# A conformer/SSD block on one core: the re-ordered hand-over with adding loads for block sums, and two token tiles transposed with the identity

## The chip, the core and the metric

The kernel runs on one core of a Trainium2 chip. The core has a matrix engine (TensorE, "PE" in the profile, with its weight loads "PEld"), and three engines for element-wise work: VectorE (DVE), ScalarE (ACT) and GpSimd (POOL). SyncE (SP), ScalarE and GpSimd also issue transfers (DMAs), each in its own queue. Each engine takes its instructions in a fixed order, and an instruction waits for semaphores that others raise. The metric is the device time of one execution in microseconds (us).

## The reference, cut to what matters

The block normalises x, mixes it in two branches (a convolution and a state-space scan), projects the mix with `w_out`, adds it to x, and then runs the feed-forward part. All data are float32: 512 tokens, width 1024, hidden width 2816. Only the seam between the projection and the feed-forward part is touched:

```python
mixed = (g_conv * conv_out + g_ssm * ssm_out) @ w_out[i]
x = x + rms_norm(mixed, mix_post_g[i])
h = rms_norm(x, ffn_pre_g[i])
gt, up = jnp.split(h @ w_gate_up[i], 2, axis=-1)
f = (jax.nn.silu(gt) * up) @ w_down[i]
x = x + rms_norm(f, ffn_post_g[i])
```

## The kernel before

**Precision.** Every large product is made of three matmuls on split numbers: each operand is a "hi" half (a cast to fp32r, ScalarE) and a "lo" half (the rest, a subtraction on VectorE). `mm3` (line 184) issues hi x hi, hi x lo and lo x hi. A lo half can be made another way: ScalarE writes the negated hi half, and GpSimd issues a transfer that adds the weight from memory to it (`halve`, line 927, for the blocks named in `ADD_LO`, line 78; the profile shows it as `wlo_g<-in_w` on POOL).

**Weights.** `w_raw` (line 142) loads pieces of 128 x 1024 (512 KB) in the order of `ORDER` through SP, into a ring of five tiles (`raw`) and later two more (`raw2`). A piece is loaded when a tile of the ring is free.

**The output projection.** `tm_wo` sums 512 tokens in four token tiles t = 0 to 3 of 128, each in two PSUM banks; the operand lies in the tiles m0h, m0l (tokens of t = 0, 1) and m1h, m1l (t = 2, 3) of the pool `mp`. The loop over `steps` (line 1080) runs t = 0 and 1 first, then 2, then 3. After the last step of a tile comes `residual(t)` (line 991): the mean of squares (ScalarE, `mean_sq`, tiles jk), the product with the gain (VectorE, `mg`), the factor (`factor`, line 869: a sum `pm` on VectorE, then a power -1/2 on GpSimd, `rs_a`), the new x (`xr`, VectorE), its mean of squares, the second factor (`rs_b`), and a diagonal matrix `dg` = identity x factor (VectorE). `xr` is loaded and then stored for the end (`x2d`) by ScalarE's queue.

**The hand-over.** `transposed(t)` (line 1014) multiplies the eight 128 x 128 pieces of xr with dg, which scales and transposes in one go (`ptr`, line 1023). The first four results go to VectorE (`xg`), the other four to ScalarE, both times with the gain of the norm. The feed-forward product uses a Strassen-Winograd scheme on 2 x 2 blocks, so hi and lo halves (`halved`, line 1037) are made of b11, b21 (from t = 0 and 2), b22 and t1 to t4 (sums, from t = 1 and 3). In the loop, `transposed(0)` stands after step (2, 1), `transposed(1)` after (2, 5) and `transposed(2)` after (3, 5).

**The block sums.** The 22 column blocks u of `w_gate_up` (gate and up in turn) come as two pieces, 2u with the upper blocks a11 | a12 and 2u + 1 with the lower ones a21 | a22. `prep_a(u)` makes hi and lo of a11, a12. `prep_s(u)` (line 949) makes four sums on VectorE, s1 = a21 + a22, s3 = a11 + a21, s2 = s1 + a11, s4 = s2 + a12, s1 in a tile of its own and the others in place of the raw pieces, and then their halves.

**The products.** `first(u)` (line 1124) starts with b11, b21 and the upper blocks. For u = 0, 1, 2 it runs before `transposed(3)`, for 3 behind it. Then per u come v1 (s1 x t1), x2 (s2 x t2), v2 (s4 x b22, into the bank of v1), x3 (s3 x t3) and x4 (a22 x t4). Between two products into one bank the bank is copied out to `D_[u]`: that is `sg` for the gates and the tile `f32[:, 2f + i]` for the up half:

```python
product(V[u], u, "s1", "t1", True)
act.copy((D_[u][1] if u in D_ else begin(u)[1])[:, c2], V[u])
```

The order for the first blocks is written out: "v0 x0 v1 w0 y0", "x1 w1 z0 y1" and so on, with v = v1, x = x2, w = v2, y = x3, z = x4. The pool `fp` of f32 is opened after `mix.close()`, so its memory lies where the pool `mp` was.

**What sets the order.** A scheduler orders each engine's instructions; `not_before` adds an order without a wait, `hold` keeps the halves behind the residual's work, `tc.issue_after` sets a place behind an instruction.

## Time and profile before

| | us |
|---|---|
| median of 3 runs (1030.25 to 1030.38) | 1030.28 |
| profiled execution, its time | 1036.17 |
| profiled execution, its span | 1034.4 |
| PE busy | 1024.2 |
| VectorE busy | 814.3 |
| ScalarE busy | 609.0 |
| GpSimd busy | 96.4 |

The profiled execution is a run of its own, some 6 us longer than the timed ones. Times in a row of the timeline count from the start of the span. The number behind the start is the duration of one instruction (of all of them, where x is above 1); matmuls overlap their predecessors, so the distance between two starts says what one costs. In the groups, the form is line, engine, operation, output <- inputs.

### The profile page before, as it was taken

The page shows a single profiled execution, that of the slowest core. Times are in us where ns is not written, and L with a number is a line of the kernel's source. Part 1 is how long each engine was busy: PE and PEld are TensorE (multiplying, and loading weights), DVE is VectorE, ACT ScalarE, POOL GpSimd, SP SyncE. Part 2 cuts the span into 40 slices and gives each one's busy share as a digit, 9 for nine tenths or more (in the row PEclk, how much of TensorE's full clock was granted, in tenths as well). Part 3 has the DMA queues.
Part 4 walks back from the last instruction along what each step waited for, and adds up shares of the span by engine and source line. Part 5 has one row for each costly group of instructions (what it writes and reads, how often), then busy time and mean ns, then how long its engine had stood idle before and what let it go on. Part 6 is the DMA issues. An engine that isn't in the chain of part 4 may idle for free.

```text
span 1034.4 us, 15686 instructions
## 1 busy us (share of the span) xinstructions
PE 1024.2 (99%) x6089; PEld 890.9 (86%) x6089; DVE 814.3 (79%) x1184; ACT 609.0 (59%) x1032; POOL 96.4 (9%) x122
## 2 busy tenths in 40 slices
PE   9999999999999999999999999999999999999997
PEld 7898889888888888888888888889999999998885
DVE  7899976959594979398976455579997788799874
ACT  7655776575748464844532673366665565568552
POOL 0101101110111011101100000010000000001000
PEclk9999999999999999999999999999999999999999
DMA  8567634655546454644452223433565345469622
GB/s 298 156 164 213 165 81 140 184 157 148 135 131 163 124 157 128 163 122 122 110 133 84 82 85 99 183 105 121 167 184 157 105 143 146 123 197 278 214 82 82
DMA packets 42458, 150.82 MB, mean 146 GB/s; under 512 B 4880, under 2 KB 5904, under 8 KB 41360
## 3 DMA queue, kind: packets, MB, share of 16 engines
q1 hardware_dynamic: 30672, 104.66, 29.9%
q0 software_dynamic: 9504, 38.80, 19.0%
q10 hardware_dynamic: 2208, 6.36, 1.8%
q8 instruction: 48, 0.79, 0.3%
q14 instruction: 26, 0.21, 0.1%
HBM read 145.54 MB, written 4.26 MB: 145 GB/s over the span
## 4 chain that ended last, share of the span: by engine, by line
PE 93%; DVE 3%; ACT 2%; issue 1%; DMA 0%; POOL 0%; SPq 0%; ACTq 0%; POOLq 0%; DVEq 0%
PE xy L187 4%; PE xy L186 4%; PE xy L188 4%; PE pz L187 3%; PE pz L188 3%; PE pz L186 3%; PE pso L186 3%; PE pso L187 3%; PE pso L188 3%; PE px L188 3%; PE px L187 3%; PE px L186 3%; PE yv L187 2%; PE yv L188 2%; PE yv L186 2%; PE yd L636 2%
## 5 line engine op out<-in xcount | busy, mean ns | idle before, releaser
L152 ACT CAST whi<-raw 128x1024 fp32r<-128x1024 f32 (+2 forms) x116 | 115.0, 1003 | 157.3 <-PE pso L187 37.5
L444 DVE SCALAR_TENSOR_TENSOR a<-v,prm_t,a 128x511 f32<-128x511 f32 (+15 forms) x240 | 179.8, 752 | 16.1 <-ACT a L441 13.8
L158 DVE TENSOR_TENSOR wlo<-raw,whi 128x1024 fp32r<-128x1024 f32 (+2 forms) x76 | 85.8, 1134 | 42.8 <-ACT whi L152 42.1
L156 POOL DMA_DIRECT2D wlo<-in_w x40 | 35.7, 893 | 353.5 <-ACT wlo L155 120.9
L188 PE MATMUL pz<-whi,hlo 128*128 128x512 f32 (+2 forms) x160 | 56.3, 352 | 0.0
L187 PE MATMUL pz<-wlo,hhi 128*128 128x512 f32 (+2 forms) x160 | 56.1, 351 | 0.0
L186 PE MATMUL pz<-whi,hhi 128*128 128x512 f32 (+2 forms) x160 | 55.4, 353 | 0.0
L186 PE MATMUL px<-hhi,whi 128*128 128x512 f32 x128 | 50.2, 392 | 0.0
L186 PE MATMUL pso<-yh,whi 128*128 128x512 f32 x128 | 50.0, 393 | 0.0
L188 PE MATMUL px<-hhi,wlo 128*128 128x512 f32 x128 | 49.8, 389 | 0.0
L187 PE MATMUL px<-hlo,whi 128*128 128x512 f32 x128 | 49.8, 389 | 0.0
L187 PE MATMUL pso<-yl,whi 128*128 128x512 f32 x128 | 49.7, 390 | 0.0
L188 PE MATMUL pso<-yh,wlo 128*128 128x512 f32 x128 | 49.7, 389 | 0.0
L930 ACT CAST whi_g<-raw 128x1024 fp32r<-128x1024 f32 x40 | 41.3, 1053 | 13.7 <-PE yv L187 8.6
L528 DVE SCALAR_TENSOR_TENSOR x<-px,prm_t,x 128x511 f32<-128x511 f32 (+2 forms) x48 | 34.7, 741 | 13.8 <-ACT x L526 13.8
L935 DVE TENSOR_TENSOR wlo_g<-raw,whi_g 128x1024 fp32r<-128x1024 f32 x34 | 41.1, 1218 | 5.1 <-ACT whi_g L930 4.7
L155 ACT ACTIVATE wlo<-whi 128x1024 fp32r<-128x1024 f32 x40 | 42.2, 1055 | 0.3
L426 ACT ACTIVATE L<-L,nacs 128x128 f32<-128x128 f32 x128 | 38.8, 389 | 0.5 <-POOL L L419 0.4
L186 PEld LDWEIGHTS pz<-whi,hhi 128*128 128x128 f32 x160 | 30.2, 189 | 3.9
L187 PEld LDWEIGHTS pz<-wlo,hhi 128*128 128x128 f32 x160 | 30.2, 188 | 3.8
L188 PEld LDWEIGHTS pz<-whi,hlo 128*128 128x128 f32 x160 | 30.1, 188 | 3.7
L930 ACT CAST chi_g<-raw 128x1024 fp32r<-128x1024 f32 x24 | 24.8, 1050 | 11.4 <-PE yv L187 5.1
(656 smaller groups left out, 3344.8 us busy)
## 6 DMA issues: line engine op xcount, KB each, us to landing
raw<-in_w SPq DMA_DIRECT2D x186, 512.0 KB, 4.5
wlo<-in_w POOLq DMA_DIRECT2D x40, 512.0 KB, 6.8
L<-scr POOLq DMA_DIRECT2D x8, 1024.0 KB, 7.1
wlo_g<-in_w POOLq DMA_DIRECT2D x11, 512.0 KB, 7.1
clo_g<-in_w POOLq DMA_DIRECT2D x7, 512.0 KB, 5.3
xr<-in_x ACTq DMA_DIRECT2D x4, 512.0 KB, 4.7
x2d<-xr ACTq DMA_DIRECT2D x4, 512.0 KB, 2.9
xres<-x2d SPq DMA_DIRECT2D x4, 512.0 KB, 3.7
```

The source lines that it names most:

```text
L152: act.copy(hi[:, c], src[:, c])
L155: act.activation(lo[:, c], hi[:, c].bitcast(F32), AF.Copy, scale=-1.0)
L156: mark["lo"] = pool.dma_start(lo[:, c], w[n][:, c].bitcast(F32R), accum_op=ALU.add)
L158: mark["wlo"] = dve.tensor_tensor(out=lo[:, c], in0=src[:, c], in1=hi[:, c].bitcast(F32), op=ALU.subtract)
L186: mark["pe"] = pe.matmul(ps, lh, rh, start=start, stop=False, skip_group_check=more)
L187: pe.matmul(ps, lh, rl, start=False, stop=False, skip_group_check=more)
L188: mark["pe3"] = pe.matmul(ps, ll, rh, start=False, stop=stop, skip_group_check=more)
L426: act.activation(L[:, h, c, :], L[:, h, c, :], AF.Exp, bias=nacs[:, c, HG * g + h : HG * g + h + 1])
L444: return dve.scalar_tensor_tensor(out=va[j][:, d:], in0=vs[j][:, : T - d], scalar=col("dw_w", j * KC + KC - 1 - d), in1=va[j][:, d:], op0= ...
L528: dve.scalar_tensor_tensor(out=a[:, d:], in0=ps[:, : T - d], scalar=col("ssm_w", i * KS + KS - 1 - d), in1=a[:, d:], op0=ALU.mult, op1=ALU ...
L930: a_ = act.copy(hi, src)
L935: d_ = dve.tensor_tensor(out=lo, in0=src, in1=hi.bitcast(F32), op=ALU.subtract)
```

## The change

- **Block sums by adding loads.** For u = 1 and 2, s1 is loaded (a21, `load_s1`, SP) and a22 is added to it by a transfer of GpSimd (`add_s1`); s3 is made by adding a11 to the raw lower piece (`add_s3`, GpSimd). VectorE keeps the sums s2 and s4. The lower pieces of u = 1 and 2 are no longer loaded into the ring: they go into a tile `b12`, in the memory of m1h, and s1 of u = 2 into that of m1l, both after the projection's last step. Block 4 joins `ADD_LO`.
- **Tiles 0 and 1** are scaled by ScalarE (two halves `xs`) and transposed with the identity (`pe.transpose`), without dg. Tiles 2 and 3 stay as they were.
- **The hand-over re-ordered.** Squares of tiles 1 to 3 stand behind earlier copies; hold marks are moved; `transposed(1)` is issued behind a matmul; `sums()` of tile 3 comes ahead of `begin(0)`; `begin(1)` is made early, into a tile `d1`. The second half of D_[1] is f32[:, 1], taken when v1(1) is reached; results of the up half go out through `f_out`.

In the built program the transposes of tile 1 stand ten matmuls later than before, those of tile 2 behind the last matmul of the projection instead of ten ahead of it.

```diff
-ADD_LO = (2, 3) + tuple(range(7, FF // P, 2))
+ADD_LO = (2, 3, 4) + tuple(range(7, FF // P, 2))
...
+    late = {}
...
-        if n < len(ORDER) and n not in raws:
-            if more_raw and n >= GU[0] and n % 7 < 2:
+        if n < len(ORDER) and n not in raws and late.get(n, True) is not None:
+            if n in late:
+                raws[n] = late[n]
+            elif more_raw and n >= GU[0] and n % 7 < 2:
...
-        pool.tensor_tensor(out=rs, in0=m, in1=neg_half[:, :1], op=ALU.pow)
+        mark["pow"] = pool.tensor_tensor(out=rs, in0=m, in1=neg_half[:, :1], op=ALU.pow)
...
+    s1s = {}
+
+    def load_s1(u):
+
+        if u == 1:
+            s1s[u] = w2.tile([P, T], F32, tag="s1", bufs=2, name=f"s1_{u}")
+        else:
+            s1s[u] = mp.tile([P, T], F32, tag="m1l", name=f"s1_{u}")
+        nc.sync.dma_start(s1s[u], w[seq["gu", 2 * u + 1]][:, :T])
+
+    def add_s1(u):
+
+        return pool.dma_start(s1s[u], w[seq["gu", 2 * u + 1]][:, T:], accum_op=ALU.add)
+
+    def add_s3(u):
+
+        return pool.dma_start(g_raw(u, 1)[:, :T], w[seq["gu", 2 * u]][:, :T], accum_op=ALU.add)
...
-        s1_ = w2.tile([P, T], F32, tag="s1", bufs=2, name=f"s1_{u}")
-        sum_ = dve.tensor_tensor(out=s1_, in0=a21, in1=a22, op=ALU.add)
+        if u in s1s:
+            s1_ = s1s[u]
+        else:
+            s1_ = w2.tile([P, T], F32, tag="s1", bufs=2, name=f"s1_{u}")
+            sum_ = dve.tensor_tensor(out=s1_, in0=a21, in1=a22, op=ALU.add)
+            if u == 3:
+                not_before(sum_, mark["t4"][1])
+            dve.tensor_tensor(out=a21, in0=a11, in1=a21, op=ALU.add)
+        sum_ = dve.tensor_tensor(out=a11, in0=s1_, in1=a11, op=ALU.add)
         if hold:
             not_before(sum_, hold[1])
-        dve.tensor_tensor(out=a21, in0=a11, in1=a21, op=ALU.add)
-        dve.tensor_tensor(out=a11, in0=s1_, in1=a11, op=ALU.add)
         dve.tensor_tensor(out=a12, in0=a11, in1=a12, op=ALU.add)
...
+            if u == 0:
+                hold[1] = mark["dg"]
             halve(("s3", "a22"), u, rb_, pair_of_tiles())
...
+    b12_raw = [seq["gu", 2 * u + 1] for u in (1, 2)]
+    late.update({n: None for n in b12_raw})
...
             ss.append(mean_sq(ps[n], pbp, f"a{t}", n))
-            m = dve.tensor_tensor(out=mg[:, c], in0=ps[n], in1=gpost0[:, c], op=ALU.mult)
-        if t == 3:
-            hold += [mark["sq"], m]
+            if t:
+                not_before(mark["sq"], mark["xg" if t > 1 else "xs"])
+            dve.tensor_tensor(out=mg[:, c], in0=ps[n], in1=gpost0[:, c], op=ALU.mult)
+        first_sq = mark["sq"]
...
+        if t == 3:
+            hold += [first_sq, m]
         rs = factor(ss, f"b{t}")
-        dg = pbp.tile([P, P], F32, tag="dg", name=f"dg{t}")
-        mark["dg"] = dve.tensor_scalar(out=dg, in0=ident, scalar1=rs, scalar2=None, op0=ALU.mult)
-        xrs[t] = xr, dg
+        if t < 2:
+            xs = [w2.tile([P, T], F32, tag=tg, bufs=2, name=f"xs{t}_{tg}") for tg in ("dhi", "dlo")]
+            for n, c in enumerate(cols2):
+                mark["xs"] = act.activation(xs[n], xr[:, c], AF.Copy, scale=rs)
+            xrs[t] = xs
+        else:
+            dg = pbp.tile([P, P], F32, tag="dg", name=f"dg{t}")
+            mark["dg"] = dve.tensor_scalar(out=dg, in0=ident, scalar1=rs, scalar2=None, op0=ALU.mult)
+            xrs[t] = [xr[:, c] for c in cols2]
+            dgs[t:] = [dg]
...
-                m = pe.matmul(pt[:, k, :], xr[:, c], dg, start=True, stop=True)
+                src = xrs[t][n][:, k * P : (k + 1) * P]
+                if t < 2:
+                    m = pe.transpose(pt[:, k, :], src, ident)
+                else:
+                    m = pe.matmul(pt[:, k, :], src, dgs[t], start=True, stop=True)
...
         if (t, k) == (2, 5):
-            sums, others = transposed(1)
+            with tc.issue_after(mark["pe"].ins):
+                sums, others = transposed(1)
             sums()
...
+        if (t, k) == (3, 2):
+            load_s1(1)
+        if (t, k) == (3, 6):
+            not_before(add_s1(1), mark["pow"])
...
-        if e == 0:
+        if u == 1:
+            d1 = h2e.tile([P, T], F32, tag="d1", bufs=1, name="d1")
+            D_[u] = [d1, None]
+        elif e == 0:
...
+    room = mp.tile([P, 2, 1024], F32, tag="m1h", name="b12")
+    for i, n in enumerate(b12_raw):
+        late[n] = room[:, i]
+        w_raw(n)
+    load_s1(2)
     halves()
-    hold[1] = mark["pm"]
     mark["chain"] = True
     for u in range(3):
         first(u)
         if u == 0:
+            hold[1] = mark["pm"]
             halves = prep_s(1)
+    for u in (1, 2):
+        not_before(add_s3(u), mark["pow"])
+    add_s1(2)
     sums, rest = transposed(3)
...
+    sums()
     begin(0)
-    sums()
     rest()
+    begin(1)
...
+    def f_out(u, i):
+        return f32[:, u - 1 + i, :] if u % 2 else D_[u][i]
...
         product(V[u], u, "s1", "t1", True)
+        if u == 1:
+            D_[u][1] = f32[:, 1, :]
         act.copy((D_[u][1] if u in D_ else begin(u)[1])[:, c2], V[u])
...
-            dve.tensor_tensor(out=d, in0=d, in1=sg[f][0], op=ALU.mult)
+            dve.tensor_tensor(out=f_out(u, 0), in0=d, in1=sg[f][0], op=ALU.mult)
```

More of the change, by code (lines that the diff above doesn't have):

```diff
@@ L1005, in residual @@
         for n, c in enumerate(cols2):
-            dve.scalar_tensor_tensor(out=xr[:, c], in0=mg[:, c], scalar=rs, in1=xr[:, c], op0=ALU.mult, op1=ALU.add)
+            m = dve.scalar_tensor_tensor(out=xr[:, c], in0=mg[:, c], scalar=rs, in1=xr[:, c], op0=ALU.mult, op1=ALU.add)
             ss.append(mean_sq(xr[:, c], pbp, f"b{t}", n))
+        if t == 3:
+            hold += [first_sq, m]
         rs = factor(ss, f"b{t}")
-        dg = pbp.tile([P, P], F32, tag="dg", name=f"dg{t}")
-        mark["dg"] = dve.tensor_scalar(out=dg, in0=ident, scalar1=rs, scalar2=None, op0=ALU.mult)
-        xrs[t] = xr, dg
+        if t < 2:
[8 more added lines that the diff above has]
+            dgs[t:] = [dg]
         nc.scalar.dma_start(x2d[t * P : (t + 1) * P, :], xr)
@@ L1016, in transposed @@
         tok = slice((t // 2) * P, (t // 2 + 1) * P)
-        xr, dg = xrs[t]
         xg = []
@@ L1021, in transposed @@
             for k in range(KB):
-                c = slice((KB * n + k) * P, (KB * n + k + 1) * P)
-                m = pe.matmul(pt[:, k, :], xr[:, c], dg, start=True, stop=True)
+                src = xrs[t][n][:, k * P : (k + 1) * P]
[3 more added lines that the diff above has]
+                    m = pe.matmul(pt[:, k, :], src, dgs[t], start=True, stop=True)
                 if t >= 2:
@@ L1034, in transposed @@
                 for k in range(KB):
-                    act.activation(xg[n][:, k], pt[:, k], AF.Copy, scale=prm_t[:, FPG + KB + k : FPG + KB + k + 1])
+                    mark["xg"] = act.activation(
+                        xg[n][:, k], pt[:, k], AF.Copy, scale=prm_t[:, FPG + KB + k : FPG + KB + k + 1]
+                    )
         def halved(name, src, sign=1.0):
@@ L1173, in x3 @@
         f, e = u // 2, u % 2
-        d = D_[u][1][:, c2]
+        d, to = D_[u][1][:, c2], f_out(u, 1)[:, c2]
         product(X[u], u, "s3", "t3", False)
@@ L1179, in x3 @@
         else:
-            gated_by(d, d, sg[f][1][:, c2])
+            gated_by(to, d, sg[f][1][:, c2])
     def v2(u):
@@ L1198, in x4 @@
         else:
-            gated_by(d, X[u], sg[f][1][:, c1])
+            gated_by(f_out(u, 1)[:, c1], X[u], sg[f][1][:, c1])
     def gated_by(out_, src, by):
```

## The prediction

> **What bounds the kernel now.** I read the page's totals first, then the busy time by stretch around the change, then the waits of TensorE (PE).
>
> ```profile
> span 1034.4 us, 15686 instructions
> PE 1024.2 (99%) x6089; PEld 890.9 (86%) x6089; DVE 814.3 (79%) x1184; ACT 609.0 (59%) x1032; POOL 96.4 (9%) x122
> ...
> 710.00:715.00 5.00, 4.58 (x40) 4.39 (x40) 4.90 (x10) 3.55 (x8) 0.00 (x0) 1.00 0.02 3
> ...
> 735.00:785.00 50.00, 50.00 (x427) 50.00 (x426) 47.20 (x72) 31.84 (x49) 1.75 (x2) 1.00 0.60 176
> ```
>
> The columns after the stretch are its length and the busy time of PE, weight load, VectorE (DVE), ScalarE (ACT), GpSimd (POOL). PE is the bound nearly everywhere: from 735 on it has no gap. Only at the hand-over from the output projection to the feed-forward part (about 697 to 729 us) does it stand, and there VectorE is the full engine (4.90 of 5.00). So a microsecond that PE loses or gains up to 729 stays to the end, and one saved on another engine counts only if PE had waited for it.
>
> ```profile
> PE xy L186 <- DVE f L1107: 0.8, 2, 0.4
> PE v L187 <- DVE t1l L1041: 0.4, 1, 0.4
> ```
>
> Those are the plain waits after 697 us. They are small, so the change has little to win and its new waits decide.
>
> **Part 1: two tiles transposed with the identity.**
>
> ```profile
> 585.96 1.13 PE L804 MATMUL pv<-ident,lxn 128*128 128x128 f32 x8
> ...
> 693.76 1.95 PE L1023 MATMUL ptr<-dg,xr 128*128 128x128 f32 x16
> 695.46 0.48 PE L188 MATMUL tm_wo<-whi,m1l 128*128 128x512 f32 x1
> ```
>
> A tile now costs 16 passes and 1.70 us of PE (693.76 to 695.46). The layer norm's transposes by the identity are the same operation on the same shape: 8 are 8 passes, 1.13 us with the tail of the last (0.28), so 0.85. Two tiles save 2 x 0.85 = 1.70 us. In return ScalarE scales two halves per tile (about 0.52 each) and VectorE drops two diagonals. The scaled halves of tile 0 fit before PE arrives, and those of tile 1 too, because their transposes stand ten matmuls later in the new order; I cost them at nothing. If the factor of tile 1 came more than about 0.7 us late, PE would wait for the excess.
>
> **Part 2: tile 2's transposes move behind the last matmul of the output projection.** Before, they stood ten matmuls ahead of it, and their copies ran under those.
>
> ```profile
> 697.60 0.39 PE L188 MATMUL tm_wo<-whi,m1l 128*128 128x512 f32 x1
> ...
> 698.18 0.39 PE L187 MATMUL xy<-b11l,a01h 128*128 128x256 f32 x1
> ...
> 699.66 0.28 PE L187 MATMUL xy<-b21l,a01h 128*128 128x256 f32 x1
> ...
> 694.85 0.69 DVE L1030 TENSOR_TENSOR xg<-ptr,prm_t 128x512 f32<-128x512 f32 x1 [0.78 <-PE ptr L1023]
> 697.43 0.69 DVE L1041 TENSOR_TENSOR b11l<-xg,b11h 128x512 fp32r<-128x512 f32 x1 [1.89 <-ACT b11h L1040]
> ...
> 695.75 1.14 ACT L1035 ACTIVATE xg<-ptr,prm_t 128x128 f32<-128x128 f32 x4 [2.17 <-PE ptr L1023]
> 696.76 0.64 ACT L1040 CAST b11h<-xg 128x512 fp32r<-128x512 f32 x1
> 697.27 0.65 ACT L1040 CAST b21h<-xg 128x512 fp32r<-128x512 f32 x1
> 697.79 0.62 ACT L866 ACTIVATE jk_a<-tm_wo 128x512 bf16<-128x512 f32 x1
> ```
>
> Durations here are distances between starts. The projection ended at 697.60 + 0.23 = 697.83. It now ends 1.70 (part 1) and 1.70 (tile 2 moved out) earlier: 694.43. From there: xg on VectorE 1.09 later (693.76 to 694.85) = 695.52; b11h 0.67 to 0.7 later (a hand-over of 512 columns, 696.76 to 697.43, taken the same in the other direction) = 696.2. ScalarE's new order is b11h 0.51, the four xg pieces 1.01, a sum of squares 0.6, then b21h: 698.3. Its lo half on VectorE follows 0.67 later (699.0), PE 0.75 after that (697.43 to 698.18): 699.75. Before, PE passed this matmul at 699.66. All 1.70 us of part 1, and the 1.70 moved, are spent waiting here: **+0.1 us**.
>
> **Part 3: the adding loads.** For u = 1 and 2 the sums s1 and s3 are made by transfers that GpSimd issues. In the built program's order the add into s1 of u = 2 stands on GpSimd ahead of the factor (pow) of tile 3's first norm, and it waits for the plain load of s1, which SP issues third after the projection's end, behind two loads of 512 KB, because all three land in the projection's operand.
>
> ```profile
> L416 POOL DMA_DIRECT2D L<-scr x8 | 4.5, 559 | 24.4 <-PE yd L636 10.6 <-DVE B L528 10.4 <-DMA scr<-scratch 3.5
> ...
> L933 POOL DMA_DIRECT2D wlo_g<-in_w x6: 858/883/916, 690.6 to 873.0; - x6
> ...
> L874 POOL TENSOR_TENSOR rs_a<-pm_a,neg_half x4: 539/698/1627, 667.1 to 700.2; 128x1 f32<-128x1 f32 x4
> ...
> xr<-in_x ACTq DMA_DIRECT2D x1, 512.0 KB, 7.2
> ...
> raw<-in_w SPq DMA_DIRECT2D x2, 512.0 KB, 5.6
> ```
>
> The first row shows GpSimd idle ahead of a transfer it issues until another transfer lands, so what is queued behind waits too: that pow, VectorE's xr behind it, the whole VectorE queue, then dg and tile 3's transposes. The load is issued at 694.43 + 0.2 + 2 x 0.33 = 695.3. The trace has no such load; the nearest rows are five raw loads close together (5.6 us, issued 656 to 657) and the residual tile's load beside two adds (7.2, issued 691.6). I take the middle, 6.4: it lands at L = 701.7; ends are 3.6 (a load by itself) and 8.0 (an add beside others).
>
> ```profile
> 701.89 1.41 DVE L1006 SCALAR_TENSOR_TENSOR xr<-mg,rs_a,xr 128x512 f32<-128x512 f32 x2 [0.46 <-POOL rs_a L874]
> 703.22 0.68 DVE L935 TENSOR_TENSOR dlo<-s,dhi 128x512 fp32r<-128x512 f32 x1
> 703.82 1.22 DVE L935 TENSOR_TENSOR clo_g<-raw,chi_g 128x1024 fp32r<-128x1024 f32 x1
> 704.96 0.20 DVE L873 TENSOR_SCALAR pm_b<-ss_b,ss_b 128x1 f32<-128x1 f32 x1
> ...
> 706.23 0.28 PE L188 MATMUL xy<-b21h,wlo_g 128*128 128x256 f32 x1
> 706.59 2.02 PE L1023 MATMUL ptr<-dg,xr 128*128 128x128 f32 x16
> ```
>
> From L: hand-over 0.1, issue of the add 0.88, pow 0.55 (nothing runs on VectorE beside it; the 1.63 is beside a lo half), 0.05, then xr 1.33, a lo half of 1024 columns 1.14 and one of 512 0.60 (now ahead of pm_b), pm_b to tile 3's transposes 1.63 (704.96 to 706.59): L + 6.3 = 708.0. PE would be there at 699.75 + 6.68 = 706.4 (699.66 to 706.23 is 6.57 for 58 matmuls, 0.113 each, and one more). Before: 706.59. So tile 3's transposes start at P = 708.0, **+1.4 us**; ends -0.15 (landing by 700.1, PE decides) and +3.0 (8.0 us, P = 709.6). The re-ordering inside the factor alone, without this wait, would have brought pm_b forward.
>
> The Trainium skill, "SBUF — State Buffer", section "SBUF: two separate sides", warns that a transfer issued from GpSimd can be starved of descriptors while VectorE holds the shared port: about 620 ns alone, about 3100 ns overlapped. The row above has six adds between 858 and 916 ns in a stretch where VectorE is nearly full, so I use 0.88; by the rule the add would take 2.2 us more and the time would be 1036.0 by estimate.
>
> **Part 4: where v of u = 1 is put.** With the new D_, the copy of v(1) goes into f32[:, 1], whose memory lies under the tile that now holds u = 2's lower blocks ("b12"), and in the built program it waits for the last reader, VectorE's lo half of that tile; on ScalarE it also stands behind two casts, the activation-table load and a Silu. The next product into that bank waits for the copy.
>
> ```profile
> 718.81 0.41 DVE L1107 TENSOR_TENSOR f<-xy,f 128x256 f32<-128x256 f32 x1
> 719.14 0.68 DVE L959 TENSOR_TENSOR raw<-raw,raw 128x512 f32<-128x512 f32 x1
> 719.28 0.39 PE L186 MATMUL xy<-t2h,chi_g 128*128 128x256 f32 x1 [0.42 <-DVE f L1107]
> 720.76 0.28 PE L186 MATMUL v<-b22h,chi_g 128*128 128x256 f32 x1
> 728.89 0.38 PE L186 MATMUL xy<-t4h,chi_g 128*128 128x256 f32 x1 [0.42 <-DVE f L1107]
> ...
> 715.71 1.05 ACT L930 CAST chi_g<-raw 128x1024 fp32r<-128x1024 f32 x1
> 716.67 0.37 ACT L1164 COPY sg<-xy 128x256 f32<-128x256 f32 x1
> 721.35 1.28 ACT L1188 ACT_TABLE_LOAD   x1
> 722.64 0.63 ACT L1188 ACTIVATE sg<-sg 128x512 f32<-128x512 f32 x1
> ```
>
> VectorE in the new order, counted from P: dg ends at P - 0.2, then a lo half 1.14, a sum 0.60, a lo half 0.60, so tile 3's xg starts at P + 2.15. From xg through the lo half of "b12": 14 operations of 512 columns at 0.60 (8.40), five of 256 at 0.33 (718.81 to 719.14; 1.65), four lo halves of 1024 at 1.14 (4.56), 14.6 in all: P + 16.8. ScalarE's way: the last sum of block 2, 11.1 into that list, is ready at P + 13.25; two casts 0.96 each (715.71 to 716.67), table 1.28, Silu 0.63, 0.1 of hand-over give P + 17.1. The copy starts at the later one, and PE's product (v, b22 of u = 1) 0.47 after it (as 718.81 to 719.28): P + 17.6. Before it began at 720.76 = 14.2 after the transposes: +3.4. PE's own work up to there is 1.78 + 96 x 0.113 = 12.7, so it stands 4.9 us.
>
> Of this something comes back: before, the next 60 matmuls (6.8 us) took 8.1 (720.76 to 728.89), because PE waited for VectorE's adds. Now VectorE has run on meanwhile: to the add that frees t4 of u = 1 it needs P + 16.8 + 7.1 (six operations of 512 and one product of 512 at 0.60, two lo halves of 1024 at 1.14, two of 256 at 0.33) = P + 23.9, and 0.47: P + 24.4, just when PE is there. Before: 728.89 = 22.3 after. Net **+2.1 us**. The adding loads save VectorE four sums (2.4) and one lo half (1.14); that is inside this count and is why it isn't worse.
>
> **Sum.** Tile 3's transposes are at +1.4 us (parts 1 to 3 together, the +0.1 of part 2 included), part 4 adds +2.1: +3.5 us. Behind 729 PE has no gaps to fill or lose. The profiled execution took 1036.17 us (span 1034.4), 5.9 above the median of 1030.28; the stage's rows differ by 0.6% at most for that, 0.02 us on this sum. So 1030.28 + 3.5 = **1033.8 us**.
>
> **The rivals.**
> 1. *The load of s1 lands early* (by 700.1): GpSimd is not late and only part 4 is left, -0.15 + 2.1: 1032.2. For it: 3.6 us of a lone load. Against: 1.25 MB start at once beside two adds.
> 2. *Faster: the place of v(1) is free in time.* If VectorE reached the end of "b12" by P + 12.7, PE would meet no wait; with P = 706.4 it would also lose before's waits from 706.59 to 728.89 (22.3 against 1.78 + 156 x 0.113 = 19.4, 2.9 us): 1030.28 - 0.15 - 2.9 = 1027.2. VectorE's list would have to be 4.1 us shorter than its rows; against it, VectorE was at 4.90 of 5.00 here. It also needs the factor in time.
> 3. *Starved adds*, as the rule has it: 1036.0, and more if the later adds hold the first pieces of "b12".
> 4. *The identity saves no passes*: everything up to P is 1.7 later, 1035.5. Against it, 8 passes for 8 transposes.
>
> **How the numbers follow.** Forecast 0.53, rival 1 0.24, rival 2 0.12, rivals 3 and 4 together 0.11. What tells from no change is 0.2%, about 2.1 us. Rival 1 lies on that line, half of it counts as same (0.12), with 0.03 of the forecast's lower tail and 0.01 of rival 2's: same 0.16. Faster 0.11, slower 0.73. The range 1030.6 to 1036.4 leaves out rival 2 and about half of rivals 3 and 4; its lower part holds rival 1 with part 4 shorter by up to 1.6, its upper the 8.0 us landing (1035.4) and rival 4.
>
> **What would show it.** PE's waits should name the copy of v(1) (ScalarE) with about 4 us at one place, and tile 3's transposes should wait for dg. The pow of tile 3 should stand right behind an adding transfer on GpSimd that starts after 701. Tiles 0 and 1 should have 8 passes each, and the first b21l matmul should come near 699.7. If no wait over 2 us stands before the product v<-b22, part 4 is wrong, and with it the forecast.

## The result and the profile after

| | before | after | ratio |
|---|---|---|---|
| median of the timed runs, us | 1030.33 (1030.25 to 1030.39, 4 runs) | 1044.68 (1044.44 to 1044.75, 4 runs) | 1.0139 (95% interval 1.0121 to 1.0156) |
| predicted | | 1033.8 (1030.6 to 1036.4) | |

The change costs 14.35 us, 10.9 more than forecast and 8 above the upper end of the range. TensorE's two longest waits of the kernel after (line waited for: us in total, times, longest; `ACT f L1236` is the copy of v(1) into f32[:, 1]):

```profile
PE ptr L1065 <- issue: 6.1, 1, 6.1
PE v L189 <- ACT f L1236: 3.8, 1, 3.8
```

The two places are the forecast ones: tile 3's transposes, and the product that needs the copy of v(1). But the first stand (time in which TensorE is idle), forecast at 1.6 us (TensorE there at 706.4, the transposes at 708.0), is 6.1 us. Its origin is in the timeline of the same kernel (start, duration, engine; in brackets the idle time ahead and what ended it; `b` are the two 512 KB loads into b12, `s` is s1):

```profile
695.19 0.86 SPq L151 DMA_DIRECT2D b<-in_w  x2
696.14 0.43 SPq L960 DMA_DIRECT2D s<-in_w  x1
...
707.54 0.87 POOL L964 DMA_DIRECT2D s<-in_w  x1 [11.24 <-DMA s<-in_w]
708.11 0.88 POOL L877 TENSOR_TENSOR rs_a<-pm_a,neg_half 128x1 f32<-128x1 f32 x1
...
713.73 3.75 PE L1065 MATMUL ptr<-dg,xr 128*128 128x128 f32 x16 [6.10 <-issue]
717.13 0.56 PE L189 MATMUL xy<-b11h,whi_g 128*128 128x256 f32 x1
...
733.45 0.58 PE L189 MATMUL v<-b22h,chi_g 128*128 128x256 f32 x1 [3.77 <-ACT f L1236]
738.73 0.41 PE L189 MATMUL xy<-t3h,chi_g 128*128 128x256 f32 x1
```

and in its transfers (the issuer, their number, KB, us from issue to landing):

```profile
s<-in_w SPq DMA_DIRECT2D x1, 256.0 KB, 10.7
```

GpSimd idles 11.24 us until the plain load of s1 has landed (696.14 + 10.7 = 706.8), issues the add, and only then makes tile 3's factor (pow); TensorE follows at 713.73. From the transposes to the next product it takes 3.40 us for 16 passes (713.73 to 717.13), about twice what it took before. The stretches tell why; the columns are busy time of PE, weight load, DVE, ScalarE and GpSimd, the granted clock, DMA share, GB/s:

```profile
704.00:708.00 4.00, 3.63 (x33) 3.43 (x31) 0.00 (x0) 0.00 (x0) 0.46 (x1) 1.00 0.29 109
...
712.00:716.00 4.00, 2.27 (x11) 2.30 (x12) 3.56 (x8) 0.09 (x1) 2.64 (x3) 0.53 0.78 224
716.00:720.00 4.00, 4.00 (x24) 4.00 (x24) 2.56 (x5) 2.48 (x8) 0.00 (x0) 0.62 0.86 201
...
736.00:740.00 4.00, 4.00 (x22) 4.00 (x22) 3.85 (x6) 3.72 (x5) 0.00 (x0) 0.56 0.13 37
```

From 704 to 708 DVE and ScalarE do nothing: the pow holds the chain of the whole hand-over. And behind each of the two stands the granted clock is 0.53 to 0.62 on average: 4 us without a gap hold 24 and 22 matmuls, where a variant below, at full clock, has 37.

The profile of before that the prediction used ran 6 us longer than the timed runs, because its 256-column matmuls stood wider apart (last section). So the traces below are held against a second profile of the same kernel, whose run took 1029.79 us. Its timeline:

```profile
706.47 2.02 PE L1023 MATMUL ptr<-dg,xr 128*128 128x128 f32 x16
...
720.65 0.28 PE L186 MATMUL v<-b22h,chi_g 128*128 128x256 f32 x1
...
728.78 0.38 PE L186 MATMUL xy<-t4h,chi_g 128*128 128x256 f32 x1 [0.50 <-DVE f L1107]
```

Each product has the same place in both orders, so the difference of its starts is the time lost so far (a product is 12 matmuls of 256 columns):

| place | before, again | after | lost so far |
|---|---|---|---|
| first projection matmul | 648.79 | 649.90 | +1.11 |
| first product (b11 of u=0) | 697.71 | 697.71 | 0.00 |
| third product | 700.79 | 702.02 | +1.23 |
| tile 3's transposes | 706.47 | 713.73 | +7.26 |
| two products on | 711.15 | 720.91 | +9.76 |
| v<-b22 of u=1 | 720.65 | 733.45 | +12.80 |
| xy<-t2 with whi_g, three products on | 725.06 | 740.49 | +15.43 |
| from xy<-t3 with whi_g on | 730.27 | 744.57 | +14.30 |

From 744 on nothing is added up to 816.

### The profile page after: what moved, and what is told of

The parts are those of the page before. It is cut to its first block, busy times and chain, and to the rows that moved or that the text cites. A ratio compares the mean times of both kernels' runs of the same rounds, so it can differ in the third digit from the quotient of the medians.

```text
span 1042.7 us, 15672 instructions
## 1 busy us (share of the span) xinstructions
PE 1021.6 (98%) x6073; PEld 887.5 (85%) x6073; DVE 813.2 (78%) x1177; ACT 611.8 (59%) x1037; POOL 100.1 (10%) x127
## 4 chain that ended last, share of the span: by engine, by line
PE 87%; DVE 6%; ACT 3%; issue 2%; DMA 0%; SPq 0%; POOL 0%; ACTq 0%; DVEq 0%; POOLq 0%
PE xy L190 4%; PE xy L189 4%; PE xy L191 4%; PE pso L189 3%; PE pso L190 3%; PE pso L191 3%; PE pz L190 3%; PE pz L191 2%; PE px L191 2%; PE px L189 2%; PE px L190 2%; PE pz L189 2%; PE yv L191 2%; PE yv L190 2%; PE yv L189 2%
## 5 line engine op out<-in xcount | busy, mean ns | idle before, releaser
L531 DVE SCALAR_TENSOR_TENSOR x<-px,prm_t,x 128x511 f32<-128x511 f32 (+2 forms) x48 | 34.7, 743 | 14.3 <-ACT x L529 14.3
L938 DVE TENSOR_TENSOR wlo_g<-raw,whi_g 128x1024 fp32r<-128x1024 f32 x32 | 38.7, 1221 | 5.3 <-ACT whi_g L933 5.2
```

Of the source, the lines that this page charges most:

```text
L531: dve.scalar_tensor_tensor(out=a[:, d:], in0=ps[:, : T - d], scalar=col("ssm_w", i * KS + KS - 1 - d), in1=a[:, d:], op0=ALU.mult, op1=ALU ...
L938: d_ = dve.tensor_tensor(out=lo, in0=src, in1=hi.bitcast(F32), op=ALU.subtract)
```

## The experiments

Four causes were to be told apart: the add ahead of the pow (part 3), the place of v(1) (part 4), the half clock, and whatever else stays when these are gone. The kernel before, repeated with the variants on each chip, had medians of 1030.69 to 1031.05. The times of the variants scatter more than those of the two kernels of the result; the two spacings in the last section fit much of that.

### The kernel before, profiled again

No edit.

> The kernel before, unchanged, with a new profile. The first profile of it took 1036.17 us against a median of 1030.3, and its matmuls of 256 columns stood 0.117 us apart from about 720 us on, against 0.113 in the profile of the change. If that was a disturbance of the one profiled execution, this one takes 1030.3 (span about 1028.6) with 0.113 throughout, and the hand-over itself (tile 3's transposes at 706.6, waits of 0.4 us) looks the same. If it belongs to the kernel, the profile again shows 0.117 and 1036.

1029.79 us. The row for the stretch that the prediction quoted with 427 matmuls is

```profile
735.00:785.00 50.00, 50.00 (x443) 50.00 (x442) 48.66 (x76) 31.58 (x49) 1.75 (x2) 1.00 0.62 183
```

16 more matmuls in the same 50 us. The hand-over itself is the same to 0.12 us (706.47 against 706.59).

### The add behind the pow

```diff
-    add_s1(2)
+    not_before(add_s1(2), mark["pow"])
```

> The change, with the add into s1 of u = 2 put behind the powers of tile 3 on GpSimd; nothing else moves. Theory (GpSimd stands 11.2 us at that add until the plain load lands, VectorE and TensorE stand behind it, and the long idle also halves TensorE's clock for a while): tile 3's transposes start at 706.5 to 707.5 instead of 713.7, their 16 passes take 1.7 instead of 3.4 us, the next product has no slow start: -9 to -9.7 us, 1035.0 to 1035.7. The wait for the copy of v(1) stays, 4 to 5 us, with its slow clock behind it. Rival (VectorE's queue or the DMA traffic sets tile 3's transposes, the add is only the last to arrive): they start at 711 or later and the time stays above 1040.

1041.13 median (1034.72 to 1042.39, 4 runs); the profiled one took 1034.72. The other three lie 6 to 8 us above it, about as far as the two spacings of the last section lie apart, but no trace of them was kept, so the reading rests on the one trace. Its timeline:

```profile
701.36 0.56 POOL L877 TENSOR_TENSOR rs_a<-pm_a,neg_half 128x1 f32<-128x1 f32 x1 [5.17 <-DVE pm_a L876]
...
707.34 1.95 PE L1065 MATMUL ptr<-dg,xr 128*128 128x128 f32 x16
709.04 0.36 PE L189 MATMUL xy<-b11h,whi_g 128*128 128x256 f32 x1
724.80 0.58 PE L189 MATMUL v<-b22h,chi_g 128*128 128x256 f32 x1 [3.46 <-ACT f L1236]
```

The pow waits for its own operand only, the transposes start at 707.34 without a wait and at full speed, and the loss from 735 on is 4.3 to 4.6 us instead of 14.3. Part 3's mechanism is shown, with the half clock behind it: 9.7 of the 14.3 us. The stand of part 4 is there alone, 3.46 us, with the half clock behind it.

### A place of its own for v(1)

A tile of 1 KB in the pool h2e takes the copy, instead of f32[:, 1]:

```diff
-            D_[u] = [d1, None]
+            D_[u] = [d1, h2e.tile([P, HB], F32, tag="d1b", bufs=1, name="d1b")]
...
-        if u == 1:
-            D_[u][1] = f32[:, 1, :]
-        act.copy((D_[u][1] if u in D_ else begin(u)[1])[:, c2], V[u])
+        d = D_[u][1] if u in D_ else begin(u)[1]
+        act.copy(d if u == 1 else d[:, c2], V[u])
...
```

> The change, with the copy of v(1) (256 columns) in a tile of its own instead of f32[:, 1], so that it need not wait for the last reader of b12; the add stays where it is. Theory: tile 3's transposes still at 713.7 with the slow clock, but no wait of 3.8 us ahead of v<-b22 of u = 1 and no second stretch of slow clock (28 matmuls at 0.213 instead of 0.113, 2.8 us): -5.5 to -6.7 us, 1038.0 to 1039.2. Rival (VectorE is the bound behind tile 3's transposes, so that the wait only moves to the next add): less than 2 us gained, 1043 or more.

1044.17 median (1042.84 to 1050.86, 4 runs): nothing gained; the expectation missed and its rival came true. TensorE's waits:

```profile
PE ptr L1065 <- issue: 6.4, 1, 6.4
PE xy L189 <- ACT d L1228: 2.0, 1, 2.0
PE xy L189 <- DVE f L1156: 1.8, 1, 1.8
```

The wait for the copy of v(1) is gone, as intended: v<-b22 starts 14.95 us behind the transposes (729.01 against 714.06) instead of 19.72. But everything else that DVE, ScalarE and the adding transfers had to do behind the late pow is as late as before, so TensorE meets it two products on. As long as part 3 stands, part 4 costs nothing of its own in this trace: the two are not additive.

### Both undone

> Both edits together. Theory: the two costs add up, 1044.7 - 9.4 - 6.1 = 1029 us, between 1028 and 1030.3, so about at the kernel before or a little below it: the two misplaced waits are the whole loss. Rival (the rest of the change, adding loads and re-ordering, costs time by itself): 1032 or more.

1035.79 median (1034.04 to 1039.41, 4 runs): missed; even the lowest is 3.7 us above the range, and the rival came true. On top of the add behind the pow, the place of its own for v(1) gave only 0.7 us (1034.72 to 1034.04, the two profiled runs). Both stands are gone; the two largest that are left:

```profile
PE xy L189 <- ACT d L1228: 1.9, 1, 1.9
PE xy L191 <- DMA wlo_g<-in_w: 1.5, 1, 1.5
```

ScalarE copies x2(1) at 725.44, behind a wait of 2.30 us for DVE's block sums, two casts, the table load and two Silus. The adding transfer into wlo_g of u=4 is new in the change (ADD_LO got a 4). The kernel before had neither wait. These two were not in my count of what the change does beyond parts 3 and 4. The trace is also 1.08 us behind at tile 3's transposes, but it was 1.19 us behind when the projection began; so the place of tile 2's transposes costs only what part 1 gains. All three are tried one by one below.

### TensorE kept busy in its two stands

```diff
+    def fill(n, bank_no, name):
+        ps, m = yd_tile(bank_no, name), mov["b11"][0][:, 0]
+        for _ in range(n):
+            d = pe.matmul(ps[:, :HB], m[:, :P], m, start=True, stop=True)
+            not_before(d, mark["pe3"])
+            mark["pe3"] = d
...
+    fill(52, 7, "fill_a")
     sums, rest = transposed(3)
...
+        if u == 1:
+            fill(48, 1, "fill_b")
         product(V[u], u, "s4", "b22", False)
```

> The changed kernel with 52 unused matmuls of 256 columns (52 x 0.1133 = 5.9 us) put on TensorE where it stands 6.1 us ahead of tile 3's transposes, and 48 (5.4 us) where it stands 3.8 us ahead of the product v<-b22 of u=1. Clock theory: the half speed behind each stand (16 passes in 3.40 us instead of 1.70, 256-column matmuls 0.213 us apart) comes from the standing itself, so it goes: tile 3's transposes still start at 713.7 but take 1.70; v<-b22 still starts near 733.4, because the copy that it waits for hangs on DVE and ACT and not on TensorE, and its 12 matmuls take 1.36 instead of 2.7. Worth 2.2 to 2.5 us: 1042.2 to 1042.5; if the copy's chain follows TensorE as well, 4.7 us: 1040. Rival (the half speed has another cause, such as the transfers): 1044.7 and the 0.213 us stays.

1049.05 median (1043.97 to 1049.68, 4 runs); the profiled one took 1043.97. The other three lie 5 us above it, about what the wider spacing costs, but no trace of them was kept. Timeline:

```profile
714.70 2.02 PE L1072 MATMUL ptr<-dg,xr 128*128 128x128 f32 x16 [0.30 <-PE fill_a L1024]
716.48 0.36 PE L189 MATMUL xy<-b11h,whi_g 128*128 128x256 f32 x1
...
734.46 0.28 PE L189 MATMUL v<-b22h,chi_g 128*128 128x256 f32 x1
737.28 0.28 PE L189 MATMUL xy<-t3h,chi_g 128*128 128x256 f32 x1
```

and a stretch, columns as above:

```profile
736.00:740.00 4.00, 4.00 (x37) 4.00 (x36) 3.93 (x6) 3.24 (x5) 0.36 (x1) 1.00 0.31 69
```

The clock stays at 1.00 behind v<-b22, the transposes take 1.78 us, and 24 matmuls from v<-b22 to xy<-t3 take 2.82 us instead of 5.28 (733.45 to 738.73). So the half speed comes from the standing itself, and the rival (the transfers) is out. v<-b22 still starts 19.76 us behind the transposes, against 19.72: the half clock of the first stand is swallowed by the second wait, and only the one behind v<-b22, 2.46 us, reaches the end. The time of the profiled run fell by less (0.5 us, 1044.44 to 1043.97): against the second profile of before, tile 3's transposes stood 1.0 us later here (0.5 of it lost ahead of the projection), some of the matmuls behind had the wider spacing, and a wait of 0.52 us followed at 754.92.

### The load of s1 at the front of SP's queue

```diff
+    load_s1(2)
     for i, n in enumerate(b12_raw):
         late[n] = room[:, i]
         w_raw(n)
-    load_s1(2)
```

> The changed kernel with the plain load of s1 for u=2 (256 KB) issued on SP's queue ahead of the two 512 KB loads for b12 instead of behind them. Place theory: the 10.7 us from issue to landing are mostly the two loads ahead of it; alone at the front it lands in 4 to 7.5 us, by 700 to 702.7, the add goes out at once, the pow of tile 3 runs at 701.5 to 703.5 and tile 3's transposes start at 707.3 to 709 instead of 713.7; the wait for the copy of v(1) stays, as in the run that had the add behind the pow: 1034.5 to 1037 (1041 with the slower spacing of matmuls that three of that run's four executions had). Rival (all transfers of this stretch share the bandwidth, the place in the queue counts little): the load lands in 9 us or more, transposes at 711.5 or later, 1041.5 to 1044.7.

1041.23 median (1036.64 to 1045.06, 8 runs). First the load among its transfers, then the timeline:

```profile
s<-in_w SPq DMA_DIRECT2D x1, 256.0 KB, 7.0
```

```profile
710.02 2.02 PE L1065 MATMUL ptr<-dg,xr 128*128 128x128 f32 x16 [1.67 <-issue]
711.80 0.37 PE L189 MATMUL xy<-b11h,whi_g 128*128 128x256 f32 x1
...
728.07 0.38 PE L189 MATMUL v<-b22h,chi_g 128*128 128x256 f32 x1 [3.90 <-ACT f L1236]
```

The place theory's landing (4 to 7.5 us) came, and tile 3's transposes are 1.0 us later than its range: 3.7 of the 10.7 us were the two loads ahead, 7.0 are left with the queue empty ahead of it. After this stand of 1.67 us the clock isn't halved (16 passes in 1.78 us). Part 4's stand is there in full, 3.90 us.

### The same, with one adding transfer less beside it

In addition, the preparation for u=3 with its adding transfer (512 KB into wlo_g) moves from step (3, 2) to behind this load.

> The changed kernel with the load of s1 for u=2 at the front of SP's queue, and with the preparation for u=3 moved behind it, so that the adding transfer of 512 KB into wlo_g (issued 695.4 to 696.2 in the other runs) isn't in flight with it. With the load in front its landing took 7.0 us instead of 10.7. Contention theory: the rest is shared bandwidth, mostly with that adding transfer: it lands in 4 to 5.5 us, and the wait of 1.67 us ahead of tile 3's transposes goes: transposes 1.5 us earlier than in that run, and the fast executions near 1035 instead of 1036.6. Rival: the load takes 7 us there whatever runs beside it: 1036.6 or more.

1036.97 median (1036.55 to 1042.79, 4 runs): the lowest misses by 1.5 us, and the landing lies between the two theories (4 to 5.5 us, and 7):

```profile
s<-in_w SPq DMA_DIRECT2D x1, 256.0 KB, 5.9
```

and its timeline:

```profile
707.37 2.02 PE L1065 MATMUL ptr<-dg,xr 128*128 128x128 f32 x16
710.93 0.39 PE L191 MATMUL xy<-b11h,wlo_g 128*128 128x256 f32 x1 [1.30 <-DMA wlo_g<-in_w]
...
726.20 0.58 PE L189 MATMUL v<-b22h,chi_g 128*128 128x256 f32 x1 [3.68 <-ACT f L1237]
```

The adding transfer into wlo_g beside it was worth 1.1 us (7.0 to 5.9, one trace each); the transposes no longer wait. TensorE stands 1.30 us for the moved transfer instead, which now lands late, and 3.68 us at part 4's place. What makes up the other 5.9 us wasn't tried: in both traces the adding transfer for s1 of u=1 was issued 1.4 to 1.5 us ahead of the load and was still under way, and the two 512 KB loads followed it. 3.6 us is the shortest landing that the prediction had seen.

### Part 1 alone

The kernel before, with tiles 0 and 1 scaled by ScalarE and transposed with the identity, and nothing else.

> The kernel before with part 1 alone: tiles 0 and 1 scaled by ScalarE and transposed with the identity, nothing else. Theory: two tiles save 0.85 us each on a TensorE that never stands there, and up to half of it is given back to the waits of 0.3 to 0.5 us at 711.8 to 728.8: 1.0 to 1.7 us below the kernel before of the same job, so 1028.8 to 1029.8 if that stands at 1030.5 to 1030.8. Rival 1: ScalarE's four scalings of 128x512 delay its casts and the whole is taken back: 1030.5 or more. Rival 2: the 1.0 us that every changed kernel so far loses at 213 us (a DVE instruction of 2.22 us there that took 0.73 before) comes with any edit: 1029.8 to 1030.3.

1033.77 median (1030.02 to 1037.61, 12 runs); the six lower ones lie at 1030.0 to 1031.7. No gain. Each tile's transposes have 8 passes, as in the changed kernel, but behind the projection TensorE stands for ScalarE (rows of ScalarE, then TensorE):

```profile
695.32 2.01 ACT L932 ACTIVATE wlo_g<-whi_g 128x1024 fp32r<-128x1024 f32 x2
...
698.91 0.38 PE L186 MATMUL xy<-b11h,a01h 128*128 128x256 f32 x1 [0.91 <-ACT b11h L1049]
```

The scalings changed ScalarE's order: two scaled copies (2.01 us) now stand ahead of tile 2's evictions; before they were done by 693.5. The trace shows rival 1 of this run, and rival 2 as well: the loss near 213 us is here too (0.88 us). Against the second profile of before, it is 1.52 us behind when the projection begins and 1.91 behind at tile 3's transposes.

### Part 1 alone, ScalarE's order mended

The preparation for u=3 moves behind the projection's last step.

> The kernel before with part 1 alone, and with the preparation of a11 and a12 for u=3 (two casts and one scaled copy of 128x1024 on ScalarE, one adding transfer) moved behind the projection's last step, so that ScalarE casts b11h of tile 2 right behind its evictions. ScalarE theory: in the run with part 1 alone TensorE gave its 1.7 us back in waits of 0.91 and 0.34 us for b11h and b11l, because ScalarE had 2.0 us of scaled copies ahead of them; those waits go, tile 3's first mean square runs 1 us earlier, and the fast executions come 1.0 to 1.3 us lower: 1028.8 to 1029.7 against 1030.0 to 1031.7. Rival: the chain of tile 3 or the later casts take it back: 1030 or more.

1036.83 median (1035.6 to 1037.42, 6 runs): about 3 us above part 1 alone, for a reason of my edit.

```profile
705.75 1.95 PE L1032 MATMUL ptr<-dg,xr 128*128 128x128 f32 x16
709.98 0.39 PE L188 MATMUL xy<-b11h,wlo_g 128*128 128x256 f32 x1 [2.05 <-DMA wlo_g<-in_w]
716.62 0.58 PE L186 MATMUL v<-t1h,dhi 128*128 128x256 f32 x1 [3.85 <-ACT t1h L1049]
...
710.14 0.69 DVE L956 TENSOR_TENSOR s<-raw 128x512 f32<-128x512 f32 x1 [5.42 <-DMA raw<-in_w]
```

b11h came in time and the transposes of tile 3 started 0.72 us earlier than in the kernel before, although this trace was 0.90 us behind when the projection began. So 1.62 of the 1.70 us that part 1 was to save are there at that place. But the later preparation freed its raw blocks later, the next load into them landed at 710.12 instead of 704.84, DVE stood 5.42 us for it, and TensorE 2.05 and 3.85 us. Whether part 1 alone can be made to gain is left open.

### Tile 2's transposes ahead again

On top of both undone, the projection's last six matmuls wait for tile 2's transposes (`mark["ptr2"]` is their last one):

```diff
-            mm3(ps[t][n], ah, al, wh[:, c], wl[:, c], k == 0, k == nk - 1)
+            m = mm3(ps[t][n], ah, al, wh[:, c], wl[:, c], k == 0, k == nk - 1)
+            if mark.get("ptr2") and k == nk - 1:
+                not_before(m, mark["ptr2"])
...
```

> The kernel with both undone (add behind the pow, v(1) with a place of its own), and with the projection's last six matmuls held behind tile 2's transposes, so that the transposes stand six matmuls ahead of the end as they did before (there ten). dg of tile 2 comes at 694.3, so TensorE stands 0.4 to 0.5 us there; b11h is then ready before TensorE needs it, and the three waits of 0.54, 0.34 and 0.43 us go: tile 3's transposes at 706.6 instead of 707.5. If that carries through: 0.9 us below the run with both undone, 1033.1 against 1034.0 for a fast execution. Rival: the later waits of that run (1.9 us for ACT's copy into d, 1.5 us for an adding transfer into wlo_g) take it back: 1034.0, with those waits longer by as much.

1033.82 median (1031.61 to 1042.24, 10 runs). The transposes of tile 3 start at 706.37, 0.10 us before those of the kernel before (both undone: +1.08). Of this 1.18 us, 0.46 are no merit of the edit: this trace was 0.73 us behind when the projection began, that one 1.19. Nine products on, TensorE is 1.09 us ahead (both undone: 0.22 behind). Then the rival comes true:

```profile
724.68 0.38 PE L189 MATMUL xy<-t3h,chi_g 128*128 128x256 f32 x1 [2.02 <-ACT d L1231]
...
729.14 0.28 PE L189 MATMUL v<-t1h,dhi 128*128 128x256 f32 x1
```

2.02 us for ScalarE's copy, then 24 matmuls in 4.46 us instead of 2.7: behind this stand, too, the clock was halved.

### ScalarE's copy ahead of the Silus

On top of that, v2(0) and x3(0) only note their Silus, and x2(1) issues them behind its copy:

```diff
-        act.copy(D_[u][0][:, c2], X[u])
+        m = act.copy(D_[u][0][:, c2], X[u])
+        if u == 1:
+            for silu in later:
+                not_before(silu(), m)
...
```

> The run with tile 2's transposes ahead, and with ScalarE's copy of x2(1) put ahead of the two Silus of u=0 (and the table load that comes with them) instead of behind. Order theory: the copy then runs near 722.8 instead of 725.3, the product xy<-t3h of u=1 no longer waits 2.0 us for it, and the half-speed stretch behind that stand (some 1.1 us) goes too: 2.5 to 3 us below the run with tile 2's transposes ahead, so its lowest time of 1031.6 becomes 1028.6 to 1029.5, below the kernel before (1030.5). Rival: DVE and the adding transfer into wlo_g are as late as the copy was, TensorE stands for them instead (over 1.5 us for wlo_g near 740): 1031 or more.

1033.54 median (1031.53 to 1039.5, 12 runs): no gain in the time, but the trace is 1.70 us ahead of the kernel before from 728 to 737, and loses 5.4 at one place (the timeline):

```profile
727.09 0.38 PE L189 MATMUL xy<-t4h,chi_g 128*128 128x256 f32 x1
...
740.60 0.39 PE L191 MATMUL xy<-b11h,wlo_g 128*128 128x256 f32 x1 [3.48 <-DMA wlo_g<-in_w]
```

The copy's wait is gone; the adding transfer for u=4 takes its place (9.8 us from issue to landing), with the half clock behind it.

### u=4 out of ADD_LO

```diff
-ADD_LO = (2, 3, 4) + tuple(range(7, FF // P, 2))
+ADD_LO = (2, 3) + tuple(range(7, FF // P, 2))
```

> The run with ScalarE's copy ahead of the Silus, and with u=4 taken out of ADD_LO, so that DVE subtracts the low half of its a11 (1.2 us) as in the kernel before, instead of ScalarE copying it and an adding transfer of 512 KB finishing it. In that run TensorE stood 1.7 us ahead of the kernel before from 728 to 738 (product xy<-t4 at 727.09 against 728.78), and lost it in one wait of 3.48 us for that transfer (9.8 us from issue to landing) and the half speed behind it. Transfer theory: both go and the 1.7 us stay: fast executions of 1028.6 to 1029.5, below the kernel before (1030.3 to 1031.2). Rival: DVE, busy without a gap from 718 to 731, passes the 1.2 us on to the block sums behind it and TensorE waits for those: 1030.5 to 1032.5.

1029.23 median (1028.59 to 1035.12, 11 runs; a twelfth took 1127.16 at a granted clock of 0.849 and is in no number here). The longest wait of TensorE in the hand-over, and a row of the timeline:

```profile
PE xy L189 <- ACT sg L1233: 0.4, 1, 0.4
```

```profile
737.82 0.28 PE L189 MATMUL yv<-b21h,whi_g 128*128 128x256 f32 x1
```

At 737.82 it is 1.97 us ahead of the kernel before (739.79). Seven of its runs lie at 1028.59 to 1029.72, where the kernel before has eleven at 1030.14 to 1031.30 on the same chip; four at 1033.9 to 1035.1, where that has six at 1036.4 to 1037.9. If the two groups are the two spacings (the profiled run, 1034.24, has the wider one from 741 on; of the others no trace was kept), this version is 2 to 2.7 us faster than before at the same spacing. The grouping was made after the runs were seen, and the interval over both groups together, 0.9949 to 1.0002, just includes no change. So the gain is seen in the trace and likely in the time, but not shown clear of the scatter.

## Why the prediction was wrong

Sum of the prediction +3.5 us, trace +14.3. The rest, term by term:

- **Part 3, the step that failed: the landing of the load of s1 (6.4 us, ends 3.6 and 8.0).** It took 10.7: +4.3, and beyond the upper end. The mechanism (the pow behind the add behind the load) was right, and the price of all that follows it was near: 6.3 us from landing to transposes forecast, 6.9 measured (+0.6). Of my two rows, the 5.6 us were of loads issued 1.13 us apart, with no adding transfer under way, and the 7.2 us of a load alone in its queue beside two adds. This load had both against it: it stood close behind 1 MB in its own queue (3.7 us by experiment) and beside adding transfers (1.1 us for one of them). I took the middle of two rows that each had a part of it, where the parts add up; with the place mended the load took 7.0 us, near the 7.2 of the second row. What makes up 5.9 of the 10.7 us stays open.
- **A term left out: the clock.** A stand was priced at its length. The trace of before had no stand over 1.0 us, so it could not show the price, and the forecast had one of 4.9 us in it all the same. The half clock cost +2.6 us behind v<-b22; that behind the transposes (2.5) ran into the second wait and cost nothing more. The Trainium skill, "TensorE: Matmul & The Clock Gate", section "Part 1: The HAM clock gate", has TensorE's clock halved after an idle window of about 3.4 us until a window as long has been busy. The granted clock agrees in kind: it was 0.50 for 6.83 us from 712.23 and from 732.71 on, two windows of 3.41 us each, and the filled stands show that the standing is the cause. Applied to the 4.9 us, this rule of the Trainium skill would have added at least half a window, some 1.7 us by estimate.
- **Part 4: right in kind, 2.1 us short.** v<-b22 was forecast 17.6 us behind the transposes and came 19.72 behind. With the pow in time it was 17.46 (724.80 - 707.34): the count of DVE and ScalarE was right for the case it assumed. Its stand was forecast at 4.9 us and is 3.77, as the transposes ahead of it ran at half speed. But its worth of +2.1 us as a separate term was wrong: taken away alone it gave nothing, and on top of part 3's edit 0.7 us.
- **Parts 1 and 2: +0.1 forecast, and nothing lost.** b21l's matmul came at 700.65 against 699.55 in the second profile of before, +1.10, and +1.11 had been lost before the projection began. 8 passes per tile are shown, 0.79 us each. That ScalarE's scalings cost nothing held in the changed order only; alone they took the gain back.
- **+1.1 us ahead of the projection**, in stages the change does not touch: the trace was 0.35 us behind at 150 us already, and lost 0.65 more near 213 (next but one section). About 0.1 us of the whole stays unassigned.
- **Rivals.** 1 (early landing) went the other way. 2 (faster, if v(1)'s place were free in time) named the right ceiling, but the late pow, tile 2's transposes, ScalarE's copy and the adding transfer for u=4 stood in the way as well; with all of them gone the trace is 1.97 us ahead at 740, where this rival had 2.9 and more. 3 (starved adds): the add took 0.87 us, those beside a busy DVE up to 1.37, so the 2.2 us more of this rival were not seen. 4 (no passes saved): refuted.
- **The signs I named** came: the wait for the copy of v(1), the pow behind an add after 701, 8 passes, b21l near 699.7 (700.65, with 1.1 us lost before). The profile puts the wait of tile 3's transposes down to "issue" and not to dg, but dg (VectorE, 713.34, 0.29 us) ends just ahead of them (713.73). The signs show the mechanism and are blind to its size.

## What to carry to other kernels

Before an instruction is put on an in-order queue ahead of one on the critical chain, ask what it waits for, and price that wait by transfers with the same place in their queue and the same traffic beside them. Price a stand of TensorE of 3.4 us or more at its length and 1.1 to 2.6 us more for the half clock behind it, as in these traces; one of 2 us may cost the same or nothing. When several engines share one late chain, removing the wait at its end can gain nothing, as here: undo the earliest first, and read from the trace which wait ends last then.

## What was not expected of the hardware

**Two spacings of the same matmuls.** A run of 256-column matmuls without a gap settles at 0.1133 or at 0.1178 us from start to start, at a granted clock of 1.00, and mostly keeps that until the next gap (in three variants it changed within a run, near 706, 727 and 728). In the first profile of before it is 0.1178 from 729 to 920, in the second 0.1133 up to 910, and the same 1619 matmuls take 6.3 us less. That fits the times: 27 runs of the kernel before on one chip fall into 22 at 1029.7 to 1031.9 and five at 1036.6 to 1038.0 with none between, and variants whose order differs by one edge scatter by 6 us. Only the profiled runs show their spacing. What decides it was not found.

**When the clock falls.** Stands of 3.46 us and more were all followed by half speed (that of 3.90 us, with s1 at the front, only after 12 matmuls at full speed), those up to 1.87 us never; of three of 2.02 to 2.05 us two were and one was not. The granted clock in the traces orders this. It changes only in steps of 3.41 us: each stretch of half clock ahead of the last 10 us is 3.41 or 6.83 us long. So a trace can be cut into windows of 3.41 us at the times of these changes. Three of them, from the run with s1 at the front (columns as above):

```profile
722.66:726.08 3.42, 1.51 (x14) 1.31 (x12) 3.42 (x6) 2.24 (x3) 0.00 (x0) 1.00 0.15 61
726.08:729.49 3.41, 1.42 (x12) 1.42 (x13) 3.41 (x6) 3.30 (x7) 0.00 (x0) 1.00 0.45 154
729.49:732.90 3.41, 3.41 (x18) 3.41 (x18) 3.41 (x7) 2.53 (x3) 0.00 (x0) 0.50 0.01 2
```

TensorE was busy for 1.51 us of the first window, and the clock stayed; it was busy for 1.42 us of the second, and the clock was halved at its end. The same border holds in all 14 traces: the clock was halved at the end of ten windows, with 0 to 1.42 us busy in each, and after none with 1.51 us or more. It came back at the end of ten windows with 2.88 us or more busy, and not after four with 0 to 2.75 us. So it counts how much of a stand falls into one window: the stands of 2.02 and 2.03 us that were followed by half speed lay within one, that of 2.05 us was split between two. A threshold of 3.4 us idle, as the Trainium skill has it on the page "TensorE: Matmul & The Clock Gate", is too kind here; the section "What's actually happening" of that page says that the window runs freely, which fits the scatter. No run was made to test the border.

**A DVE instruction held by GpSimd.** The changed kernel and all eleven builds with an edit, part 1 alone among them, lose time near 203 us, though every engine's order up to 600 us is that of before. First the kernel after, then the second profile of before, DVE and GpSimd:

```profile
203.65 2.22 DVE L447 SCALAR_TENSOR_TENSOR a<-v,prm_t,a 128x504 f32<-128x504 f32 x1
...
203.32 2.01 POOL L422 TENSOR_SCALAR_AFFINE_SELECT L<-L 128x2048 f32<-128x2048 f32 x1 [7.76 <-DMA L<-scr]
```

```profile
203.31 0.73 DVE L444 SCALAR_TENSOR_TENSOR a<-v,prm_t,a 128x504 f32<-128x504 f32 x1
...
204.53 2.01 POOL L419 TENSOR_SCALAR_AFFINE_SELECT L<-L 128x2048 f32<-128x2048 f32 x1 [9.32 <-DMA L<-scr]
```

Where GpSimd's select starts first, DVE's operation takes 2.22 us instead of 0.73 (2.06 to 2.45 in the twelve builds) and ends 0.5 us behind the select; TensorE loses 0.5 to 0.9 us at 213, by the run (0.65 in the kernel after). The Trainium skill, "SBUF — State Buffer", section "Who interferes with whom", says that a DVE instruction with two inputs in SBUF shares a read port with GpSimd and that whoever issues first holds it: the rows agree. In the kernel before, DVE's operations beside the select had one input in PSUM and took their usual 0.68 to 0.74 us. The select waits for the transfer L<-scr, which landed 8.1 to 8.5 us after its issue in the twelve builds and 9.8 us in both profiles of before; why was not found.
